# The first norm's chain, the gate weights and the order of the head stages of an mLSTM and sparse-attention trunk

## The chip, the cores and the metric

The kernel runs on one core of a Trainium2 chip. The metric is the device time of one execution in microseconds (us), as the median of several runs. Engines are named by their short names in the profile: PE is TensorE, DVE is VectorE, ACT is ScalarE, POOL is GpSimd, SP is SyncE; PEld is TensorE's weight load.

## The reference, cut to what matters

Two layers work on x of 256 tokens by 1024 channels, each as x + mixer(rmsnorm(x)); a last RMSNorm follows. The change lies in layer 0, an mLSTM block with 4 heads of 512 channels:

```python
x_in, z = split(rmsnorm(x) @ w_in)               # 1024 -> 2048 + 2048
x_conv = silu(conv4(x_in) + conv_b)              # 4 taps per channel, causal
q, k, v = headwise(x_conv, w_q), headwise(x_conv, w_k), headwise(x_in, w_v)   # 4x4 blocks
gates = concat([q, k, v]) @ w_if + b_if          # 8 gates per token
hh = mlstm(q, k, v, gates); y = (layernorm(hh) * ln_w + skip * x_conv) * silu(z)
x = x + y @ w_out
```

Layer 1 is attention with compressed, selected and window branches. All of it is float32.

## The kernel before, in words

**Products.** A product of float32 matrices is made of three products of parts: each operand is split into a high part (`hi`, `hh`, which ScalarE rounds) and the rest (`lo`, `hl`, which VectorE subtracts), and high by high, high by low and low by high are added up in PSUM (`project_channels`, L402). The weights come in units of 1 MB, two halves each (`load_unit`, L258): SP's queue loads the raw half into one of four buffers `wr`, ScalarE writes the high part `wh` (L274), and the low part `wl` is either VectorE's (L280) or, for the halves in `BY_DMA`, a copy by ScalarE (L277) and an adding transfer from POOL's queue (L278). High and low parts have five buffers each. `next_unit` keeps the loads two units ahead of their use (`LOOK`), `ahead(N0)` starts them.

**The first norm.** x comes transposed in four pieces `xch0`. ScalarE and VectorE write its scaled parts (`scaled`, L340, lines L342 and L343) without the norm's factor. The squares and their sum `sq1` (L350 to L356, then L385) are shared out by `SQA` (squares on ScalarE, the others on POOL) and `SQP` (adds on POOL, the others on VectorE). `norm1` (L384) sums over the channels by a product with ones (L388), takes the mean and 1e-6 (L323), the power -1/2 on POOL (L325), spreads the result over all partitions by a product with two diagonal tiles `dg` (L377, L378) and gets the row scale `rb1` (L389) and its half `rb1h` (L390). `rb1` is first used where the first projection leaves PSUM (`evac_x`, L438). `rstd_of` and `token_rows` serve the second layer's norm too.

**Head stages.** A loop over 4 heads (L431) projects two units into `xin` (2 buffers), and then makes the products of this head: block-diagonal weights `bdq`, `bdv` by POOL from `bm`, a part of the constants `cst` (L398); the gate weights folded through the 4x4 blocks by VectorE (`gate_weights`, L461), a product (L463) and a reduction (L464) for v and for q of each head; four convolution taps (L476 to L487); then products L497 (q), L504 (v with its gate columns), L511 and L512 (scores and gates). `cst`, the gate weights `wif` and x itself are loaded after the first unit, each behind a one-element copy of `rb1` into the tile (L441 to L449), which holds the transfer back until `rb1` is there. x1, `sq1`, `xch0`, `wif` and `z` share three buffers of the tag `zt`.

**What sets the order.** Each engine and each queue takes its instructions in one order, fixed at compile time. It is not the order of the text alone: a list scheduler runs through the program with a time model and gives each engine, among the instructions that it holds ready, the one that stands first in the text. So work of a later unit may come before that of an earlier stage, and an instruction whose operands are late on the chip holds up all that stands behind it on its engine.

Of the kernel before, what the change touches and what calls it, by code (L numbers as in the profile page):

```python
# [9 lines left out]
F32 = mybir.dt.float32  # L10
# [50 lines left out]
N0 = 2  # L61
# [4 lines left out]
SQP = (1, 2)  # L66
XT = 'zt'
NOT_POOL = (0, 1, 2, 11)
BOTH = (15, 16, 17)
BY_DMA = [(i, 1) for i in list(range(24)) + list(range(24, 48, 2)) if i not in NOT_POOL] + [(i, 0) for i in BOTH]  # L70

# [131 lines left out]
def trunk(ctx, tc, a, out, dbg=None):  # L203
# [80 lines left out]
    plan = [(a["wi1"], i, KT, 256) for i in range(16)] + [(a["wo1"], i, 4, 512) for i in range(8)]  # L284
# [99 lines left out]
    def norm1():  # L384
# [46 lines left out]
    for h in range(NH):  # L431
        xin = T([P, 4, S + 3], tag="xin", bufs=2)
        GP.memset(xin[:, :, 0:3], 0.0)
        for u in range(2):
            def evac_x(ps, x_=xin[:, 2 * u:2 * u + 2, 3:], first=(h, u) == (0, 0)):
                if first:
                    norm1()
                V.tensor_tensor(x_, ps, spread(rb1), op=OP.mult)  # L438
            project_channels(a["wi1"], 2 * h + u, evac_x, ("px", "px", "acc1")[(2 * h + u) % 3])
            if (h, u) == (0, 0):  # L440
                V.tensor_copy(cst[:, 0:1], rb1[:, 0:1])  # L441
                nc.sync.dma_start(cst, a["cst"][:, 0:n_res])
                wifs = [T([P, 16, n // 128, 8], tag="zt", bufs=ZT, name="wif") for n in (1024, 512)]
                for t, o_, n in zip(wifs, (0, 1024), (1024, 512)):
                    V.tensor_copy(t[:, 0, 0, 0:1], rb1[:, 0:1])
                    nc.sync.dma_start(t.rearrange("p a b c -> p (a b c)"), a["wif"][:, o_:o_ + n])
                for i in range(2):
                    V.tensor_copy(xt[i][:, 0, 0:1], rb1[:, 0:1])
                    nc.sync.dma_start(xt[i], a["x"][:, i * 512:(i + 1) * 512].rearrange("(t p) c -> p t c", p=P))  # L449
        if h == 0:  # L450

            wqk = CA("wqk").rearrange("p (c i) -> p c i", c=16)
            wv = CA("wv").rearrange("p (c i) -> p c i", c=16)
            atmp = T([P, 16, 4, 4], tag="f4", bufs=F4, name="atmp")
            V.tensor_tensor(atmp, CA("wkrep").rearrange("p (c i j) -> p c i j", c=16, i=4),
                            wqk[:, :, 0:4, None].to_broadcast([P, 16, 4, 4]), op=OP.mult)
            AT = T([P, 16, 4], name="AT")
            V.tensor_reduce(AT, atmp.rearrange("p c i j -> p c j i"), axis=AX.X, op=OP.add)
        own = slice(4 * h, 4 * h + 4)

        def gate_weights(out, wgt, wif, nq):  # L461
            tmp = T([P, 4, nq * 4, 8], tag="wtmp", bufs=2)
            V.tensor_tensor(tmp, wif[:, own, :, :], wgt[:, own, :, None].to_broadcast([P, 4, nq * 4, 8]), op=OP.mult)  # L463
            V.tensor_reduce(out, tmp.rearrange("p c i g -> p c g i"), axis=AX.X, op=OP.add)  # L464

        bdq = blockdiag(AT[:, own, :], F32)
        bdv = blockdiag(wv[:, 4 * h:4 * h + 4, :], F32, PG)
        gate_weights(bdv[:, :, P:PG], wv, wifs[1], 1)
# [23 lines left out]
        gate_weights(q[:, :, S:SG], wqk, wifs[0], 2)  # L492
# [27 lines left out]

    ident_r = TS([P, P], F32R, name="ident_r")
# [124 lines left out]
    for h in range(NH):  # L646
        z = T([P, 4, S], tag="zt", bufs=ZT, name="z")
        for u in range(2):
# [75 lines left out]
    nc.sync.dma_start(pkb, a["pkb"])  # L724
# [419 lines left out]
```

## Time and profile before

| | us |
|---|---|
| median of 3 runs | 381.38 (380.86 to 384.1) |
| profiled execution | 378.87 |
| its span, first to last instruction | 377.1 |
| PE busy | 350.6 (93%) |
| DVE busy | 255.7 (68%) |
| ACT busy | 241.5 (64%) |
| POOL busy | 134.7 (36%) |

Times in rows are from the start of the span. Busy PE is time in which at least one product is in flight; products are pipelined, so that the time of one is longer than the distance to the next. Idle time of an engine that is not the bound costs nothing by itself. A row of the timeline may join several instructions (xN), and its duration is then that of all.

### The profile page before, as it was taken

Reading aid. Unit: us, or ns where it says so; the run is one execution under the profiler, and the core shown is the slowest. Engines: PE = TensorE matmul, PEld = TensorE weight load, DVE = VectorE, ACT = ScalarE, POOL = GpSimd, SP = SyncE. Lnnn points to the kernel's source line nnn. Section 1 sums busy time; section 2 is a strip of 40 time slices with the busy share of each in tenths; the row PEclk is TensorE's granted clock in tenths of the full one; section 3 lists DMA queues with packets and bytes.
Section 4 is the critical chain, followed back from the end, with each engine's and each line's share of the span. In section 5 each row is a group of like instructions: output and inputs, shape, how many; then the busy total and the mean of one; then the engine's idle time right before and its main releaser. Section 6 shows DMA issues by size and latency. Waiting matters only on the chain.

```text
span 377.1 us, 6621 instructions
## 1 busy us (share of the span) xinstructions
PE 350.6 (93%) x2399; PEld 313.8 (83%) x2399; DVE 255.7 (68%) x535; ACT 241.5 (64%) x438; POOL 134.7 (36%) x165
## 2 busy tenths in 40 slices
PE   6998799979999979999999799999879999999991
PEld 6998799869998968988887699999869996777771
DVE  5976999756476548983243736687979789684515
ACT  6674669738468649765653744372579789996304
POOL 5226377433301124610100303283430283857003
PEclk9999899999999999999999999999989999999997
DMA  7889758765646978999998897546577865020003
GB/s 260 280 269 315 209 129 217 188 152 125 167 157 159 197 210 217 228 233 296 239 262 239 266 343 216 173 104 155 154 195 209 246 237 158 2 56 2 2 0 112
DMA packets 21633, 69.57 MB, mean 185 GB/s; under 512 B 2528, under 2 KB 2912, under 8 KB 21600
## 3 DMA queue, kind: packets, MB, share of 16 engines
q1 hardware_dynamic: 15472, 48.71, 38.7%
q0 software_dynamic: 4752, 16.83, 24.6%
q10 hardware_dynamic: 1376, 3.61, 2.9%
q8 instruction: 19, 0.31, 0.3%
q14 instruction: 14, 0.11, 0.1%
HBM read 50.87 MB, written 1.05 MB: 138 GB/s over the span
## 4 chain that ended last, share of the span: by engine, by line
PE 39%; DMA 23%; DVE 18%; issue 8%; ACT 8%; POOL 1%; SPq 1%; ACTq 0%; POOLq 0%; DVEq 0%
PE ps L411 17%; DMA wl<-wr 7%; DMA wr<-in_wo_dram 6%; DVE xc L487 6%; PE ps L694 6%; DVE wl L280 4%; DMA wr<-in_wi2z_dram 3%; DMA wr<-in_wi2k_dram 2%; ACT wh L274 2%; PE ps L984 2%; PE ps L909 2%; PE ps L897 2%; DMA cst<-in_cst_dram 2%; DMA xch<-in_xt_dram 1%; ACT wl L277 1%
## 5 line engine op out<-in xcount | busy, mean ns | idle before, releaser
L411 PE MATMUL ps<-hT,wh 128*128 128x256 f32 x832 | 139.5, 293 | 2.4 <-DVE hT L343 1.3
L274 ACT ACTIVATE wh<-wr 128x1024 fp32r<-128x1024 f32 (+2 forms) x90 | 89.5, 1000 | 58.1 <-PE ps L411 21.5
L411 PEld LDWEIGHTS ps<-hT,wh 128*128 128x128 f32 x832 | 121.8, 198 | 4.6 <-DVE hT L343 1.9
L280 DVE TENSOR_TENSOR wl<-wr,wh 128x1024 fp32r<-128x1024 f32 (+2 forms) x57 | 70.9, 1244 | 36.0 <-ACT wh L274 33.2
L411 PE MATMUL ps<-hT,wl 128*128 128x256 f32 x416 | 87.7, 287 | 0.0
L411 PEld LDWEIGHTS ps<-hT,wl 128*128 128x128 f32 x416 | 66.4, 193 | 1.0 <-issue 0.6
L278 POOL DMA_DIRECT2D wl<-wr x33 | 28.7, 877 | 107.9 <-ACT wl L277 103.5
L277 ACT ACTIVATE wl<-wr 128x1024 fp32r<-128x1024 f32 (+1 forms) x33 | 33.8, 1025 | 13.4 <-PE ps L694 6.6
L694 PE MATMUL ps<-wh,r 128*128 128x512 f32 x128 | 41.4, 398 | 0.0
L487 DVE SCALAR_TENSOR_TENSOR xc<-xin,pka,xc 128x256 f32<-128x256 f32 x44 | 30.8, 754 | 0.1
L694 PEld LDWEIGHTS ps<-wh,r 128*128 128x128 f32 x128 | 24.0, 188 | 5.5
L694 PE MATMUL ps<-wl,r 128*128 128x512 f32 x64 | 25.3, 395 | 0.0
L694 PE MATMUL ps<-wh,y 128*128 128x512 f32 x64 | 21.8, 406 | 0.0
L803 POOL TENSOR_TENSOR swap<-swap,trig 128x512 f32<-128x512 f32 x6 | 10.2, 1697 | 18.9 <-DMA swap<-qu 7.3
L775 PE MATMUL ps<-wl,hT 128*128 128x280 f32 (+1 forms) x48 | 15.8, 330 | 1.2 <-DMA wl<-wr 1.2
L846 PE MATMUL ps<-ka,qt 128*128 128x256 f32 (+1 forms) x32 | 12.0, 380 | 3.8 <-DVE nm L852 3.7
L774 PE MATMUL ps<-wh,hT 128*128 128x280 f32 (+1 forms) x48 | 15.5, 329 | 0.0
L776 PE MATMUL ps<-wh,hT 128*128 128x280 f32 (+1 forms) x48 | 15.2, 325 | 0.0
L694 PEld LDWEIGHTS ps<-wh,y 128*128 128x128 f32 x64 | 11.8, 188 | 3.1 <-issue 0.8
L694 PEld LDWEIGHTS ps<-wl,r 128*128 128x128 f32 x64 | 12.0, 188 | 2.8 <-DMA wl<-wr 0.2
L641 POOL TENSOR_TENSOR xc<-xc,pka 128x1024 f32<-128x1024 f32 x4 | 9.8, 2455 | 12.2 <-PE ps L512 12.2
L504 PE MATMUL ps<-m,xin 128*128 128x136 f32 x64 | 9.7, 299 | 3.6 <-DVE m L464 3.5
(473 smaller groups left out, 676.0 us busy)
## 6 DMA issues: line engine op xcount, KB each, us to landing
wr<-in_wi_dram SPq DMA_DIRECT2D x34, 512.0 KB
wl<-wr POOLq DMA_DIRECT2D x31, 512.0 KB, 5.9
wr<-in_wo_dram SPq DMA_DIRECT2D x24, 512.0 KB
wr<-in_wi2k_dram SPq DMA_DIRECT2D x12, 512.0 KB
wr<-in_wi2z_dram SPq DMA_DIRECT2D x8, 512.0 KB
wr<-in_wi2v_dram SPq DMA_DIRECT2D x8, 280.0 KB
cw<-in_cw_dram ACTq DMA_DIRECT2D x4, 512.0 KB
xch<-in_xt_dram SPq DMA_DIRECT2D x4, 256.0 KB
```

The costliest lines, as they stand in the source:

```text
L274: A.activation(hi[:, k, :], raw[:, k, :], AF.Copy)
L277: A.activation(lo[:, k, :], raw[:, k, :], AF.Copy, scale=-1.0)
L278: GP.dma_start(out=lo[:, k, :].rearrange("p k n -> p (k n)"), in_=raw[:, k, :].rearrange("p k n -> p (k n)"), accum_op=OP.add)
L280: V.tensor_tensor(lo[:, k, :], raw[:, k, :], f32(hi[:, k, :]), op=OP.subtract)
L411: PE.matmul(ps[:, c, :], w, (hl if i == 1 else hh)[:, k, :], start=(k, c, i) == (0, 0, 0), stop=(k, i) == (KT - 1, 2), skip_group_check=True)
L487: V.scalar_tensor_tensor(xc[:, c, :], xin[:, c, tap:tap + S], tap_w(tap, c), xc[:, c, :], op0=OP.mult, op1=OP.add)
L694: PE.matmul(acc, l, r[:, k % 2, cols], start=first and i == 0, stop=last and i == 2)
L774: PE.matmul(o_, lh, hi[:, k % 2, :], start=kt == 0, stop=False)
L775: PE.matmul(o_, lh, lo[:, k % 2, :], start=False, stop=False)
L776: PE.matmul(o_, ll, hi[:, k % 2, :], start=False, stop=kt == KT - 1)
L803: (GP, V)[RE[1]].tensor_tensor(sw, sw, turn(1), op=OP.mult)
L846: PE.matmul(o_, lq, ka[:, g, :, 0:w_], start=True, stop=False)
```

## The change

Squares: all four on ScalarE, after the scaled parts, their adds on VectorE. `norm1` stands ahead of the first projection, and of the loads of the second unit (`N0` is 1) and of `pka`. In it the mean goes from VectorE to ScalarE, the diagonal tiles to POOL, the half to ScalarE. `cst` and `wif` are released by `sq1` in place of `rb1`; x and `pkb` are loaded in the third head's projection. The gate weights of all heads are folded at once (`fold`), with two products and two reductions on VectorE, and POOL copies each head's part. Projections (A) and products (B) of the heads become stages of their own in the order of `STAGES`. Two casts go from VectorE to POOL. `silu_z1` is there and not called.

```diff
-N0 = 2
+N0 = 1
-SQP = (1, 2)
+SQP = ()
+XTH = 2
+WI1 = range(16)
+STAGES = "A0 A1 B0 A2 B1 A3 B2 B3"
...
-        V.tensor_scalar(me, ms, 1.0 / n, 1e-6, op0=OP.mult, op1=OP.add)
+        A.activation(me, ms, AF.Copy, scale=1.0 / n, bias=1e-6)
...
-    nc.sync.dma_start(pka, a["pka"])
...
+    scaled(range(KT), lambda kt: xch0[kt // 4][:, kt % 4, :], gain1)
     sq1 = T([P, 4, S], tag="zt", bufs=ZT, name="sq1")
...
-        (A.activation(o_, x_, AF.Square) if q in SQA else GP.tensor_tensor(o_, x_, x_, op=OP.mult))
+        A.activation(o_, x_, AF.Square)
         if q:
             (GP if q in SQP else V).tensor_tensor(sq1[:, 0:2, :], sq1[:, 0:2, :], o_, op=OP.add)
-    scaled(range(KT), lambda kt: xch0[kt // 4][:, kt % 4, :], gain1)
...
-            V.tensor_scalar(dg[:, tb, :], ident, r[:, tb:tb + 1], None, op0=OP.mult)
+            GP.tensor_scalar(dg[:, tb, :], ident, r[:, tb:tb + 1], None, op0=OP.mult)
...
-        V.tensor_scalar(rb1h, rb1, 0.5, None, op0=OP.mult)
-
+        A.activation(rb1h, rb1, AF.Copy, scale=0.5)
+
+    norm1()
+    ahead(2)
+    nc.sync.dma_start(pka, a["pka"])
...
+    def heads_x(h):
+        xin = xins[h] = T([P, 4, S + 3], tag="xin", bufs=2)
         GP.memset(xin[:, :, 0:3], 0.0)
         for u in range(2):
-            def evac_x(ps, x_=xin[:, 2 * u:2 * u + 2, 3:], first=(h, u) == (0, 0)):
-                if first:
-                    norm1()
+            def evac_x(ps, x_=xin[:, 2 * u:2 * u + 2, 3:]):
                 V.tensor_tensor(x_, ps, spread(rb1), op=OP.mult)
             project_channels(a["wi1"], 2 * h + u, evac_x, ("px", "px", "acc1")[(2 * h + u) % 3])
             if (h, u) == (0, 0):
...
+                small_weights()
+        if h == XTH:
+            V.tensor_copy(pkb[:, 0:1], xin[:, 0, 3:4])
+            nc.sync.dma_start(pkb, a["pkb"])
+            for i in range(2):
+                V.tensor_copy(xt[i][:, 0, 0:1], xin[:, 0, 3:4])
+                nc.sync.dma_start(xt[i], a["x"][:, i * 512:(i + 1) * 512].rearrange("(t p) c -> p t c", p=P))
...
+    def small_weights():
+
+        wifs = [T([P, 16, n // 128, 8], tag="zt", bufs=ZT, name="wif") for n in (1024, 512)]
+        V.tensor_copy(cst[:, 0:1], sq1[:, 0, 0:1])
+        for t, o_, n in zip(wifs, (0, 1024), (1024, 512)):
+            V.tensor_copy(t[:, 0, 0, 0:1], sq1[:, 0, 0:1])
+            nc.sync.dma_start(t.rearrange("p a b c -> p (a b c)"), a["wif"][:, o_:o_ + n])
+        nc.sync.dma_start(cst, a["cst"][:, 0:n_res])
...
+        def gate_weights(wgt, wif, nq, name):
+            out = T([P, 16, 8], name=name)
+            tmp = T([P, 16, nq * 4, 8], tag="f4", bufs=F4, name="wtmp")
+            V.tensor_tensor(tmp, wif, wgt[:, :, :, None].to_broadcast([P, 16, nq * 4, 8]), op=OP.mult)
+            V.tensor_reduce(out, tmp.rearrange("p c i g -> p c g i"), axis=AX.X, op=OP.add)
+            return out
...
+    def heads_products(h):
         if h == 0:
...
+            fold()
+        xin = xins.pop(h)
...
-        gate_weights(bdv[:, :, P:PG], wv, wifs[1], 1)
+        bdq = blockdiag(folded["AT"][:, own, :], F32)
+        bdv = blockdiag(folded["wv"][:, own, :], F32, PG)
+        GP.tensor_copy(bdv[:, :, P:PG], folded["gv"][:, own, :])
...
-        gate_weights(q[:, :, S:SG], wqk, wifs[0], 2)
+        GP.tensor_copy(q[:, :, S:SG], folded["gq"][:, own, :])
...
+    for stage in STAGES.split():
+        {"A": heads_x, "B": heads_products, "Z": silu_z1}[stage[0]](int(stage[1]))
+
     ident_r = TS([P, P], F32R, name="ident_r")
-    V.tensor_copy(ident_r, ident)
+    GP.tensor_copy(ident_r, ident)
     maskt_r = T([P, 2, P], F32R, name="maskt_r")
-    V.tensor_copy(maskt_r, C("maskt")[:, None, :].to_broadcast([P, 2, P]))
+    GP.tensor_copy(maskt_r, C("maskt")[:, None, :].to_broadcast([P, 2, P]))
...
-    nc.sync.dma_start(pkb, a["pkb"])
```

## Rows read from the trace of the kernel before

**Rows 1.** Stages: start:end length, busy us (instructions) per engine, PEclk, DMA share, GB/s
```profile
6.00:14.00 8.00, 6.53 (x28) 5.94 (x29) 8.00 (x12) 7.34 (x14) 4.49 (x3) 1.00 1.00 364
14.00:36.00 22.00, 22.00 (x187) 22.00 (x186) 16.38 (x29) 12.84 (x18) 7.84 (x7) 1.00 0.85 264
36.00:40.00 4.00, 0.51 (x6) 0.34 (x4) 4.00 (x5) 0.00 (x0) 4.00 (x4) 1.00 0.69 277
40.00:46.00 6.00, 6.00 (x38) 6.00 (x39) 6.00 (x14) 4.84 (x9) 1.11 (x2) 0.72 0.87 210
...
77.00:80.00 3.00, 0.60 (x4) 0.45 (x3) 3.00 (x6) 0.00 (x0) 1.31 (x1) 1.00 0.87 187
```

**Rows 2.** TensorE's waits: line, releaser, us in total, times, longest
```profile
PE ps L504 <- DVE m L464: 3.5, 1, 3.5
PE ps L497 <- DVE gsc L516: 2.4, 1, 2.4
```

**Rows 3.** Chain of waits from 16 to 40 us: start, us, what
```profile
25.97 6.04 DMA cst<-in_cst_dram
...
32.33 4.75 DVE xc L487 x4
37.08 2.45 DVE wtmp L463 x2
```

**Rows 4.** Stages for TensorE alone: length, PE busy, PEclk, DMA share, GB/s
```profile
42.00:44.00 2.00, 2.00 (x11) 0.50 1.03 205
```

**Rows 5.** Timelines of DVE and POOL, norm chains: start, us, engine line, operation, out<-in
```profile
14.80 0.43 DVE L385 TENSOR_TENSOR sq<-sq 128x256 f32<-128x256 f32 x1
18.51 1.63 POOL L325 TENSOR_TENSOR r<-r1me,mhalf 128x2 f32<-128x2 f32 x1 [7.01 <-DVE r1me L323]
20.17 0.48 DVE L377 TENSOR_SCALAR dg<-pk,r 128x128 f32<-128x128 f32 x2 [0.61 <-POOL r L325]
24.53 0.42 DVE L389 COPY rb<-ps 128x256 f32<-128x256 f32 x1 [1.37 <-PE ps L378]
...
210.35 1.48 DVE L323 TENSOR_SCALAR r2me<-r2ms 128x2 f32<-128x2 f32 x1
```

**Rows 6.** Timelines of SP's queue and of ACT, third and fourth unit
```profile
14.19 2.53 SPq L273 DMA_DIRECT2D wr<-in_wi_dram  x2
...
20.84 1.06 ACT L274 ACTIVATE wh<-wr 128x1024 fp32r<-128x1024 f32 x1 [1.86 <-DMA wr<-in_wi_dram]
```

**Rows 7.** Single lines on VectorE: count, shortest/median/longest ns, first and last start, forms
```profile
L463 DVE TENSOR_TENSOR wtmp<-wif,pka x8: 279/413/1477, 37.0 to 49.5; 128x128 f32<-128x128 f32 x4, 128x256 f32<-128x256 f32 x4
L464 DVE TENSOR_REDUCE m<-wtmp x4: 360/366/398, 39.5 to 56.9; 128x32 f32<-128x128 f32 x4
L464 DVE TENSOR_REDUCE q<-wtmp x4: 597/634/650, 39.7 to 51.4; 128x32 f32<-128x256 f32 x4
...
L280 DVE TENSOR_TENSOR wl<-wr,wh x21: 677/1217/2804, 6.4 to 118.3; 128x1024 fp32r<-128x1024 f32 x17, 128x512 fp32r<-128x512 f32 x4
```

**Rows 8.** A small POOL line, in the same columns
```profile
L508 POOL TENSOR_TENSOR gva<-gva,v x4: 313/1040/1681, 47.6 to 91.1; 128x64 f32<-128x64 f32 x4
```

**Rows 9.** Timelines of DVE and ACT in the first 12 us
```profile
5.61 0.87 DVE L343 SCALAR_TENSOR_TENSOR hT<-xch,pk,hT 128x256 fp32r<-128x256 f32 x2
6.41 1.52 DVE L280 TENSOR_TENSOR wl<-wr,wh 128x512 fp32r<-128x512 f32 x1
7.85 1.89 DVE L343 SCALAR_TENSOR_TENSOR hT<-xch,pk,hT 128x256 fp32r<-128x256 f32 x2
9.10 0.63 ACT L354 ACTIVATE sq<-xch 128x512 f32<-128x512 f32 x1
10.27 1.90 DVE L343 SCALAR_TENSOR_TENSOR hT<-xch,pk,hT 128x256 fp32r<-128x256 f32 x2
```

**Rows 10.** Timelines of DVE and POOL before the wait at 77 us
```profile
73.40 5.99 DVE L487 SCALAR_TENSOR_TENSOR xc<-xin,pka,xc 128x256 f32<-128x256 f32 x3
75.64 2.66 POOL L534 TENSOR_TENSOR vsp<-v,vsp 128x1024 fp32r<-128x1024 f32 x1
```

More of the change, by code (lines that the diff above doesn't have):

```diff
@@ L282, in load_unit @@
         return halves
-    plan = [(a["wi1"], i, KT, 256) for i in range(16)] + [(a["wo1"], i, 4, 512) for i in range(8)]
+    plan = [(a["wi1"], i, KT, 256) for i in WI1] + [(a["wo1"], i, 4, 512) for i in range(8)]
     of_step = {"v": [(a["wi2v"], i, 4, 280) for i in range(4)], "c": [(a["wi2"], i, 4, 512) for i in range(2)]}
@@ L430, in trunk @@
     convw = CA("convw").rearrange("p (t c) -> p t c", t=4)
-    for h in range(NH):
-        xin = T([P, 4, S + 3], tag="xin", bufs=2)
+    xins, zt_ = {}, {}
+    def heads_x(h):
+        xin = xins[h] = T([P, 4, S + 3], tag="xin", bufs=2)
         GP.memset(xin[:, :, 0:3], 0.0)
         for u in range(2):
-            def evac_x(ps, x_=xin[:, 2 * u:2 * u + 2, 3:], first=(h, u) == (0, 0)):
-                if first:
-                    norm1()
+            def evac_x(ps, x_=xin[:, 2 * u:2 * u + 2, 3:]):
                 V.tensor_tensor(x_, ps, spread(rb1), op=OP.mult)
@@ L440, in trunk @@
             if (h, u) == (0, 0):
[L441 to L449, printed above, removed]
@@ L450, in trunk @@
-        if h == 0:
[L452 to L458, printed above, removed]
@@ L459, in trunk @@
-        own = slice(4 * h, 4 * h + 4)
[L461 to L467, printed above, removed]
-        gate_weights(bdv[:, :, P:PG], wv, wifs[1], 1)
+                small_weights()
@@ new lines, in heads_x @@
+        if h == XTH:
[4 more added lines that the diff above has]
+                nc.sync.dma_start(xt[i], a["x"][:, i * 512:(i + 1) * 512].rearrange("(t p) c -> p t c", p=P))
+    folded = {}
+    def small_weights():
[5 more added lines that the diff above has]
+        nc.sync.dma_start(cst, a["cst"][:, 0:n_res])
+        folded["wif"] = wifs
@@ new lines, in fold @@
+    def fold():
+        wifs = folded["wif"]
+        wqk = CA("wqk").rearrange("p (c i) -> p c i", c=16)
+        wv = CA("wv").rearrange("p (c i) -> p c i", c=16)
+        atmp = T([P, 16, 4, 4], tag="f4", bufs=F4, name="atmp")
+        V.tensor_tensor(atmp, CA("wkrep").rearrange("p (c i j) -> p c i j", c=16, i=4),
+                        wqk[:, :, 0:4, None].to_broadcast([P, 16, 4, 4]), op=OP.mult)
+        AT = T([P, 16, 4], name="AT")
+        V.tensor_reduce(AT, atmp.rearrange("p c i j -> p c j i"), axis=AX.X, op=OP.add)
+        def gate_weights(wgt, wif, nq, name):
[4 more added lines that the diff above has]
+            return out
+        folded.update(AT=AT, wv=wv, gv=gate_weights(wv, wifs[1], 1, "gwv"), gq=gate_weights(wqk, wifs[0], 2, "gwq"))
@@ L519, in trunk, with silu_z1, evac_z @@
         scs.append(sc)
+    def silu_z1(h):
+        z = zt_[h] = T([P, 4, S], name="z")
+        for u in range(2):
+            def evac_z(ps, z=z[:, 2 * u:2 * u + 2, :]):
+                V.tensor_tensor(z, ps, spread(rb1), op=OP.mult)
+                A.activation(z, z, AF.Silu)
+            project_channels(a["wi1"], 8 + 2 * h + u, evac_z)
+    for stage in STAGES.split():
+        {"A": heads_x, "B": heads_products, "Z": silu_z1}[stage[0]](int(stage[1]))
     ident_r = TS([P, P], F32R, name="ident_r")
-    V.tensor_copy(ident_r, ident)
+    GP.tensor_copy(ident_r, ident)
     maskt_r = T([P, 2, P], F32R, name="maskt_r")
-    V.tensor_copy(maskt_r, C("maskt")[:, None, :].to_broadcast([P, 2, P]))
+    GP.tensor_copy(maskt_r, C("maskt")[:, None, :].to_broadcast([P, 2, P]))
     causal = C("mask2")
@@ L646, in trunk @@
     for h in range(NH):
-        z = T([P, 4, S], tag="zt", bufs=ZT, name="z")
-        for u in range(2):
+        z = zt_[h] if h in zt_ else T([P, 4, S], tag="zt", bufs=ZT, name="z")
+        for u in range(0 if h in zt_ else 2):
             def evac_z(ps, z=z[:, 2 * u:2 * u + 2, :]):
```

## The prediction

> **What bounds the kernel now.** I read the table of stages first, cut where TensorE's idle time lies: it shows that the kernel is held by TensorE nearly everywhere (22.00 of 22.00 us between 14 and 36 us) and that three stretches of the region that the change edits have holes: 6 to 14 us (6.53 of 8), 36 to 40 us (0.51 of 4) and 77 to 80 us (0.60 of 3) [rows 1]. What an edit is worth is read from these holes. The list of TensorE's waits says what ended the two deep ones: L504 (the products of head 0 with the value weights) waited 3.5 us for the gate weights of L464, and L497 waited 2.4 us for a PSUM bank that VectorE's `gsc` add at L516 had to free [rows 2].
>
> The chain of waits through 26 to 40 us then shows why L464 was late: the 6.04 us of the `cst` load, issued at 25.97 us only, since it is held back until the row scale `rb1` exists; then 4.75 us for four convolution steps, 2.45 us for the two gate products [rows 3]. The stall has a second price. After it the granted clock is 0.72 of full speed over the six us from 40 to 46 [rows 1], with 0.50, that is 1.2 of 2.4 GHz, in all of 42 to 44 us [rows 4]; in the stretches before it is 1.00. Lost work: 6 x 0.28 = 1.7 us. So the hole before head 0 costs 3.5 + 1.7 = 5.2 us. The shorter one at 77 us was not followed by a lower clock.
>
> **The change part by part.**
>
> *Loads of `cst` and `wif` tied to the squares, behind the third unit's.* Before, both wait for `rb1`, done at 24.95 us [rows 5]; after, their gate is the sum of squares `sq1`, whose last add ended at 15.2 us [rows 5]. On SP's queue they now stand behind the third unit's second half, which issued right at 14.19 us, and ahead of the fourth unit's, which before followed at about 16 to 18 us [rows 6]. So they issue near 15 to 17 us. With `cst`'s own 6.04 us from issue to landing [rows 3] they are there at about 21 to 23 us, some 9 us sooner than 32.0. Fold, block-diagonal weights and gate copies for head 0 then need: two gate instructions and their POOL work, about 5 us, so L504's operands are ready at 27 to 30 us. TensorE comes to L504 at about 35 us, being full of units 1 to 4 until then. Margin 5 us or more: **the 3.5 us stall goes, and the 1.7 us of lower clock with it: 5.2 us.** What is late next is the fourth unit, behind 1.02 MB more (128 partitions of 1536 and 456 words). At the 264 GB/s of that stretch [rows 1] that is 3.9 us. Its first half was converted at 20.84 us [rows 6], and TensorE began that unit at about 31 us (it ran dry at 36.5, less 48 products at 187 in 22 us [rows 1]): some 10 us in hand, so I put it at nothing. Its last half is tighter, as its low part goes through a further POOL transfer; that bounds a loss at 0 to 2 us. The loads of x and `pkb` (1.1 MB) move out of this crowded stretch to the third head's, which pays part of it back.
>
> *The fold.* Eight products (0.28 and 0.41 us at their usual) and eight reductions (0.37 and 0.63 us) become four: worked out from the sizes, products at 0.68 and 1.22 us (L280 has the same sizes), reductions at about 1.2 and 2.2 us (0.63 less 0.37 per 128 elements more) [rows 7]. 5.3 us against 6.8: 1.5 us less VectorE work. More to the point, it moves from VectorE's full stretch, 36 to 57 us, into 14 to 36 us, where VectorE was busy 16.38 of 22 us [rows 1]. Eight gate copies on POOL come in, 0.31 us each at the least [rows 8], 2.5 us in all, beside the products: nothing on the path.
>
> *Squares on ScalarE, POOL's adds to VectorE.* POOL's two squares and two adds leave. Between 6 and 12 us they stretched VectorE: L280 took 1.52 us where 0.68 is its least for that size, a pair of L343 took 1.89 us where another one took 0.87, and another pair 1.90 [rows 7, 9]: 0.84 + 1.02 + 1.03 = 2.9 us lost on the engine that feeds the first products. But ScalarE, busy 7.34 of 8 us there [rows 1], gets two more squares of 0.63 us [rows 9], 1.26 us, ahead of or behind the last `hT`. Between 1.3 us lost and 1.8 us gained I take 0.8 us: the last inputs land near 9.5 us anyway, and the ordering is open, the scaled copies being emitted first.
>
> The Trainium skill (SBUF — State Buffer, Who interferes with whom) says that a VectorE instruction with two SBUF inputs and a GpSimd instruction that reads SBUF exclude each other whole, which the rows of 1.52 and 1.89 us bear out. By that rule alone the front would give back all 2.9 us instead of 0.8, and the sum would be 9.3 us.
>
> *The chain to the row scale, emitted first.* The mean and 1e-6 go to ScalarE, the two diagonal products to POOL (VectorE did them in 0.48 us [rows 5]; POOL's row for the power is 1.63 us, so 0.5 to 3.3 us), the halved copy to ScalarE. TensorE does not wait for `rb1` as such: from 14 to 36 us it is full although `rb1` comes at 24.95 us. So the earlier scale alone is worth nothing; what it brings is an earlier first convolution. The same helpers serve the second norm near 212 us, where the mean on VectorE took 1.48 us [rows 5]; moving the mean away from there and adding POOL's slower products I bound at -1 to +1 us and take 0. The two casts that go to POOL are off the path.
>
> *The order A0 A1 B0 A2 B1 A3 B2 B3.* It puts the next head's projections ahead of a head's products. TensorE's real order was already so in the first four units, so the early part is unchanged; later it gives VectorE more time per head.
>
> *The stall at 77 us.* Three convolution steps took 5.99 us beside POOL instructions that stay, one of them of 2.66 us [rows 10]. Nothing here removes them; only their place changes. Bounds 0 and 2.4 us; I take the middle, 1.2.
>
> Sum: 5.2 + 0.8 + 1.2 = 7.2 us. The profiled execution took 378.87 us, span 377.1 and 1.8 around it: 369.9 span, 371.7 us in all. The median of the runs is 381.38 us, 2.5 above that execution; on it the forecast is **374.2 us**. After 110 us TensorE is again the bound, and the weight loads follow its releases of buffers, so I let the gain pass.
>
> **Rivals.**
>
> *More goes than I count.* Front 1.8 us, both later holes whole: 5.2 + 1.8 + 2.4 = 9.4 us, 372.0 us, and to 369.5 us if the second norm's wait goes as well. For it: VectorE's load falls in all of 14 to 57 us. Against: POOL's long instructions remain.
>
> *A new wait takes the place of the old.* Either VectorE copies that release `wif` and `cst` are queued late, so that the loads hardly come sooner (then the change does not do what it says), or `wif` is late at the fold and holds up the conversions queued behind it on VectorE, as the convolution at 32.33 us came only behind `cst` [rows 3]; or the fourth unit's low half is 2 us late and the clock falls again, 1.7 us. 3 to 6 us of the 7.2 are lost: 377.4 to 380.5 us, taken as 379.
>
> *TensorE is held by the scale chain (the slower side).* L388 and L378 are now emitted ahead of the first unit's products. TensorE takes its queue in order. If L378 is queued soon after L388, everything behind it waits for ScalarE's mean, POOL's power and POOL's diagonals. Before, with these spread out, it was 9.7 us from the sum of squares (15.2) to `rb1` (24.95) [rows 5], and TensorE waited for none of it. Were all of it waited for, with 1.7 us of clock after it, that is 11.4 us against 7.2 gained: 385.6 us. Without queueing, the chain's own steps (power 1.63, diagonals 0.5 to 3.3, mean and products about 1.5) are 4 to 6 us. It makes the kernel slower from 7.2 us of waiting on. Against it: the products of unit 1 have their data in the same stretch and would have to be ordered behind for no reason.
>
> **How the numbers follow.** Chances: forecast 0.55 (its own range 371.5 to 377.5 us), more goes 0.15, a new wait 0.20, held by the scale chain 0.10. 1% is about what a measurement of this kernel can tell from no change: 377.6 and 385.2 us. Faster: the first two but a little, 0.66. Slower: half of the last and some unforeseen disorder downstream, 0.09, as the whole order of instructions is laid out anew. The same: 0.25. The range, 369.5 to 381.5 us, takes in the first three and leaves out the last and a tail.
>
> **What would show it.** Right: no wait of L504 over 1 us, granted clock 1.00 through 36 to 46 us, `cst` landed before 24 us, `rb1` before 21 us, VectorE's first L343 pairs near 0.9 us, TensorE past the last L504 some 6 to 8 us sooner. Wrong: a TensorE wait at L388, L378 or at L411 for ScalarE's copies of unit 4; a clock of 0.5 anywhere before 60 us; or the head stage's gain lost again in the waits at L615 or past 200 us.

## The result and the profile after

| | before | after |
|---|---|---|
| median of 4 runs each | 381.12 us (379.45 to 384.1) | 389.12 us (387.03 to 390.16) |
| profiled execution | 378.87 us | 388.65 us |
| its span | 377.1 us | 386.9 us |
| PE, DVE, ACT, POOL busy | 350.6, 255.7, 241.5, 134.7 us | 354.9, 247.2, 243.4, 128.4 us |

The ratio is 1.028, 95% interval 1.022 to 1.033: slower by 8 us, where 374.2 us were forecast and 381.5 was the upper end of the range. Medians are of all runs, ratios of the fast ones alone (a run counts as slow when it is over 1.5% above the fastest of its kernel; in e3 and e6 below these are two of four). Table of stages of the changed kernel, with the columns of [rows 1]: first that group's stretches, then the ones in which the time went.

```profile
6.00:14.00 8.00, 6.12 (x31) 5.92 (x32) 7.02 (x13) 7.34 (x15) 0.00 (x0) 0.61 0.96 360
14.00:36.00 22.00, 17.98 (x137) 17.81 (x137) 16.91 (x22) 13.29 (x19) 12.33 (x18) 0.89 0.83 272
36.00:40.00 4.00, 4.00 (x26) 4.00 (x26) 1.89 (x2) 1.64 (x3) 2.15 (x2) 0.68 0.88 209
40.00:46.00 6.00, 6.00 (x53) 6.00 (x52) 4.56 (x7) 5.59 (x10) 2.77 (x4) 1.00 0.58 158
77.00:80.00 3.00, 3.00 (x22) 2.79 (x21) 1.82 (x2) 2.71 (x4) 1.11 (x2) 1.00 0.75 262
84.00:104.00 20.00, 18.69 (x145) 17.93 (x144) 13.19 (x16) 10.93 (x18) 9.06 (x6) 1.00 0.36 95
160.00:200.00 40.00, 36.33 (x156) 27.92 (x155) 11.97 (x15) 22.14 (x28) 5.11 (x6) 1.00 0.95 254
210.00:220.00 10.00, 6.07 (x25) 4.70 (x24) 3.86 (x6) 6.60 (x13) 4.36 (x7) 0.80 0.93 303
```

The last three stretches of the kernel before, which the prediction did not read:

```profile
84.00:104.00 20.00, 20.00 (x155) 19.43 (x154) 10.71 (x15) 13.21 (x21) 6.15 (x6) 1.00 0.61 142
160.00:200.00 40.00, 40.00 (x182) 32.31 (x181) 18.37 (x23) 24.71 (x31) 6.00 (x7) 1.00 0.99 260
210.00:220.00 10.00, 8.36 (x54) 7.38 (x53) 6.80 (x14) 6.84 (x13) 3.19 (x5) 1.00 0.99 300
```

The reader is to see three things. The holes at 36 to 40 and 77 to 80 us are gone, but one of 4 us stands in 14 to 36. In 160 to 200 us, the out-projection, TensorE was full before (182 products) and now makes 156. And there the DMA engines were as full as TensorE already before: 0.99. The changed kernel's waits of TensorE (engine, tile, line, releaser: us in total, times, longest) name the same places:

```profile
PE ps L418 <- DVE xin L445: 4.0, 1, 4.0
PE ps L811 <- ACT hT L346: 3.9, 1, 3.9
PE ps L418 <- ACT wh L279: 3.2, 3, 1.6
PE ps L732 <- DMA wl<-wr: 2.9, 4, 1.4
```

How the time went, by the start of the first ("begins") or of the last ("ends") of TensorE's instructions of a stage (us):

| | before | after | difference |
|---|---|---|---|
| head 0's value products begin | 40.0 | 41.2 | +1.2 |
| last scores end | 100.4 | 97.3 | -3.1 |
| out-projection begins | 156.9 | 155.9 | -1.0 |
| out-projection ends | 203.2 | 206.5 | +3.3 |
| diagonals of the second norm end | 213.6 | 220.5 | +6.9 |
| second layer's keys begin | 269.1 | 280.6 | +11.5 |
| last product ends | 369.0 | 378.7 | +9.7 |

The heads were 3 us early at 97 us. The loss came later, where nothing had been edited but two helpers: 2.1 us up to the out-projection, 4.3 in it, 3.6 from there to the diagonals and 2.8 in the second layer. The prediction had named a gain lost again "past 200 us" as a sign of being wrong.

### The profile page after: what moved, and what is told of

The parts are those of the page before. It is cut to its first block, busy times and chain, and to the rows that moved or that the text cites. A ratio compares the mean times of both kernels' runs of the same rounds, so it can differ in the third digit from the quotient of the medians.

```text
span 386.9 us, 6634 instructions
## 1 busy us (share of the span) xinstructions
PE 354.9 (92%) x2399; PEld 316.8 (82%) x2399; DVE 247.2 (64%) x517; ACT 243.4 (63%) x443; POOL 128.4 (33%) x175
## 4 chain that ended last, share of the span: by engine, by line
PE 57%; DMA 16%; DVE 11%; ACT 7%; issue 6%; SPq 1%; ACTq 0%; POOLq 0%; POOL 0%; DVEq 0%
PE ps L418 27%; DMA wl<-wr 6%; PE ps L732 5%; DMA wr<-in_wi_dram 4%; DMA wr<-in_wo_dram 3%; DVE wl L285 3%; ACT wh L279 2%; PE ps L653 2%; PE ps L537 2%; PE ps L1021 2%; PE ps L946 2%; PE ps L530 2%; PE ps L934 2%; PE ps L523 2%; DMA xch<-in_xt_dram 1%
## 5 line engine op out<-in xcount | busy, mean ns | idle before, releaser
L418 PE MATMUL ps<-hT,wh 128*128 128x256 f32 x832 | 139.0, 294 | 8.6 <-DVE xin L445 4.0
L418 PEld LDWEIGHTS ps<-hT,wh 128*128 128x128 f32 x832 | 121.9, 199 | 11.1 <-issue 6.3
L285 DVE TENSOR_TENSOR wl<-wr,wh 128x1024 fp32r<-128x1024 f32 (+2 forms) x57 | 67.4, 1186 | 47.2 <-ACT wh L279 45.1
L418 PE MATMUL ps<-hT,wl 128*128 128x256 f32 x416 | 88.9, 289 | 1.1 <-ACT p__495_2879 L891 1.1
L418 PEld LDWEIGHTS ps<-hT,wl 128*128 128x128 f32 x416 | 67.6, 195 | 2.0 <-ACT p__495_2879 L891 1.5
L732 PE MATMUL ps<-wh,r 128*128 128x512 f32 x128 | 41.2, 398 | 0.8 <-DVE x L754 0.8
L513 DVE SCALAR_TENSOR_TENSOR xc<-xin,pka,xc 128x256 f32<-128x256 f32 x44 | 29.1, 723 | 4.3 <-ACT xc L502 2.5
L811 PE MATMUL ps<-wh,hT 128*128 128x280 f32 (+1 forms) x48 | 16.4, 352 | 3.9 <-ACT hT L346 3.9
L812 PE MATMUL ps<-wl,hT 128*128 128x280 f32 (+1 forms) x48 | 16.7, 350 | 0.0
L840 POOL TENSOR_TENSOR swap<-swap,trig 128x512 f32<-128x512 f32 x6 | 8.3, 1384 | 24.6 <-DMA swap<-kraw 12.6
L813 PE MATMUL ps<-wh,hT 128*128 128x280 f32 (+1 forms) x48 | 15.7, 339 | 0.0
L811 PEld LDWEIGHTS ps<-wh,hT 128*128 128x128 f32 x48 | 9.5, 201 | 5.2 <-ACT hT L346 4.4
L732 PE MATMUL ps<-wl,y 128*128 128x512 f32 x32 | 12.8, 401 | 0.0
```

The lines of the kernel that those rows point to most:

```text
L285: V.tensor_tensor(lo[:, k, :], raw[:, k, :], f32(hi[:, k, :]), op=OP.subtract)
L418: PE.matmul(ps[:, c, :], w, (hl if i == 1 else hh)[:, k, :], start=(k, c, i) == (0, 0, 0), stop=(k, i) == (KT - 1, 2), skip_group_check=True)
L513: V.scalar_tensor_tensor(xc[:, c, :], xin[:, c, tap:tap + S], tap_w(tap, c), xc[:, c, :], op0=OP.mult, op1=OP.add)
L732: PE.matmul(acc, l, r[:, k % 2, cols], start=first and i == 0, stop=last and i == 2)
L811: PE.matmul(o_, lh, hi[:, k % 2, :], start=kt == 0, stop=False)
L812: PE.matmul(o_, lh, lo[:, k % 2, :], start=False, stop=False)
```

## The experiments

Ratios are to the kernel before on the same chip, with 95% intervals (its median there: 378.36 us for e1 to e4, 378.27 for e5 to e8, 379.88 for e9 to e12, 380.6 for e13 to e16). Theories: A, the second norm's helpers cost the time; F, the order of stages and these helpers do together; H, the order by itself; S, the out-projection is bound by its weight stream; W, the early stall is the fold's wait for `wif` on VectorE's queue. The letters in the expectations that are not listed here are explained where they stand.

**e1, second norm's helpers back** (in the changed kernel)

```diff
-        A.activation(me, ms, AF.Copy, ...)
+        V.tensor_scalar(me, ms, ...) if name == "r2" else A.activation(...)
-            GP.tensor_scalar(dg[:, tb, :], ident, ...)
+            (V if place else GP).tensor_scalar(dg[:, tb, :], ident, ...)
```

> The changed kernel, but in the second norm the mean and the two diagonal tiles go back to VectorE; every engine's order ahead of that norm is the changed kernel's own. Theory A (the helpers that both norms share cost the loss at the second norm: ScalarE's mean stands behind a conversion that waits for a load, POOL's diagonals take 1.2 us, and the clock falls): TensorE's idle time near 213 to 217 us falls from about 4.9 to 1 to 2 us, no stretch at 0.50, and the kernel takes 381 to 384 us, 5 to 8 less than the changed one. Theory B (the loss comes from the weight stream being late ahead of the second norm): 387 to 389 us, TensorE still idle there, waiting for what a load brings.

Measured 388.97 us (387.91 to 392.07), 1.030 [1.022, 1.038]. The diagonals ended at 215.0 instead of 220.5 us, and the keys began at 276.4 instead of 280.6; and yet nothing reached the end: the second layer came out of the list scheduler in another order, in which the keys take 77.2 us instead of 70.9 and the values end at 373.3 instead of 370.0. A alone falls as to the total.

**e2, the helpers alone** (the same two edits the other way round, in the kernel before)

> The kernel before, but in the second norm the mean goes to ScalarE and the diagonal tiles to POOL; the order ahead of that norm is the kernel before's own. Theory A: slower than before by 5 to 8 us (386 to 389), with a longer wait of TensorE at the diagonal product of the second norm and a lower clock behind it. Theory B: 380 to 383 us.

Measured 381.82 us, 1.012 [1.004, 1.021]: the helpers cost about 1% even without the rest, not the 5 to 8 us that A had asked for.

**e3, fold per head** (the changed kernel with the old products and reductions of each head)

```diff
-            tmp = T([P, 16, nq * 4, 8], tag="f4", ...)      # all heads, once
+            tmp = T([P, 4, nq * 4, 8], tag="wtmp", bufs=2)  # one head
...
-        GP.tensor_copy(bdv[:, :, P:PG], folded["gv"][:, own, :])
+        gate_weights(bdv[:, :, P:PG], folded["wv"], wifs[1], 1)
```

> The changed kernel with the gate weights folded head by head as before (eight products and eight reductions, written straight to their places), all else of it kept. Theory C (the fold of all heads, queued on VectorE ahead of the first three projections' leaving of PSUM, costs the 4.0 us wait and the lower clock at 29 to 40 us): the wait for xin before head 0's products falls under 1.5 us, the head stage ends 4 to 6 us sooner. If what is gained there lasts: 383 to 385 us. Theory D (weight loads or the second norm decide the time behind it, so that gains of the head stage do not last): 387 to 390 us with the head stage sooner.

Measured 389.22 us (384.04 to 392.04), 1.021 [1.008, 1.034]. Head 0's value products began at 34.0 us, 7 us earlier. So the early stall is the fold's, and taking it away in this manner brings nothing that can be told from noise.

**e4, old order of the stages** (in the changed kernel)

```diff
-STAGES = "A0 A1 B0 A2 B1 A3 B2 B3"
+STAGES = "A0 B0 A1 B1 A2 B2 A3 B3"
```

> The changed kernel with the order A0 B0 A1 B1 A2 B2 A3 B3 as the loop before had it, all else kept. If the new order is what helps the head stage (its last products were 3 us sooner than before in spite of the wait at 29 us): 390 to 393 us. If it is neutral: 388 to 390. If it is what puts the fold and the weights in a bad order: 383 to 386.

Measured 381.46 us, 1.007 [1.002, 1.012]: 2% of the 2.8% come back with one line, and they do so ahead of the second layer: the diagonals of the second norm end at 211.3 us instead of 220.5. It is more than was expected, 383 us at the least.

**e5, old order and helpers back** (e4 and e1)

> The changed kernel with the old stage order and with the second norm's mean and diagonals back on VectorE. Theory F (two harmful parts, each with its own loss: the stage order some 2% and the second norm's engines some 1%, and the rest of the change gains in the head stage): 374 to 378 us against 378.4 before on this chip, ratio 0.985 to 1.00, and 3 us less than with the order alone put back. Theory G (what is put right at the second norm is lost again in the newly laid out second layer, as when it alone was put back): the same as with the order alone put back, ratio 1.00 to 1.01.

Measured 377.2 us, 0.996 [0.992, 1.000]. F holds: without these two parts the change is level with the kernel before or a little under it. Against e4 (381.46) the helpers are worth 1%, though in e1 they gave nothing.

**e6, new order alone** (the kernel before, its loop cut into A and B)

```diff
-    for h in range(NH):
+    def heads_x(h): ...
+    def heads_products(h): ...
+    for stage in "A0 A1 B0 A2 B1 A3 B2 B3".split(): ...
```

> The kernel before with nothing but the order A0 A1 B0 A2 B1 A3 B2 B3 of the head stages. Theory H (projections first bunch the use of weights and leave a stretch of two heads' products in which no weight buffer comes free, the loads pause, and the out-projection, bound by the weight stream, starts with less in hand): 1.5 to 2.5% slower than before, a stretch near 85 to 100 us with a DMA share under 0.3, and TensorE waits in the out-projection. Theory I (the order is harmful only together with the fold): within 0.7% of before.

Measured 394.7 us (388.35 to 397.18), 1.032 [1.023, 1.041]. The order alone makes the kernel before slower, by about as much as the whole change does. But only 3.7 us of it are there at the diagonals of the second norm (217.3 against 213.6 us); of the 14.6 us at the last product, 10.9 come in the second layer, which has the longer order of e1 (keys 79.1 us). H's figure for the pause, a DMA share under 0.3, was missed: 0.40.

**e7, head 0's z units between B2 and B3** (in the changed kernel; their SiLU becomes one instruction in it):

```diff
-STAGES = "A0 A1 B0 A2 B1 A3 B2 B3"
+STAGES = "A0 A1 B0 A2 B1 A3 B2 Z0 B3"
```

> The changed kernel with the first gate-path stage (two weight units, its SiLU as one function) put between the products of heads 2 and 3: weights are used in the stretch that had none. Theory H: the DMA share at 85 to 100 us rises from 0.2 to over 0.5 and 3 to 7 us are gained on the changed kernel (382 to 386). Theory J (the pause of the loads does not matter, as they are ahead of their use): within 2 us of the changed kernel's 389.

Measured 383.9 us, 1.012 [1.005, 1.019], 5 us less than the changed kernel. 84 to 104 us in e6, then in e7:

```profile
84.00:104.00 20.00, 18.70 (x141) 17.77 (x140) 13.47 (x18) 11.65 (x21) 9.53 (x7) 1.00 0.40 106
```

```profile
84.00:104.00 20.00, 20.00 (x157) 19.53 (x156) 12.88 (x13) 12.08 (x20) 7.88 (x6) 1.00 0.50 138
```

With two product stages side by side no weight buffer comes free and the loads pause: DMA share 0.40 in e6 and 0.36 after, against 0.61 before. A weight stage between them brings it to 0.50.

**e8, e5 with the fold per head**

> The changed kernel with the old stage order, the old second norm and the gate weights folded head by head. The 4 to 5 us wait of TensorE for xin at 29 to 33 us is the fold's, so that it falls under 1.5 us in any case. If the fold's wait is what is left of the loss: 2 to 5 us less than with the order and the norm alone put back, 371 to 375 us. If VectorE's backlog takes it back later, as it did in the changed kernel with its own order (TensorE's lag 7.4 us at 40 us, but 17 at 80): the same as without it, within 2 us.

Measured 386.26 us, 1.020 [1.013, 1.026]. Its out-projection began at 151.5 us, 3.3 earlier than that of e5, and ended at 202.4, 0.8 later, with three waits for `wl`; the rest of its loss lies in the second layer, which has the longer order of e1 again (keys 79.1 us). Neither expectation came: it is 2.4% over e5. Being early brought nothing. That pointed to what the out-projection is fed by. By queue in 160 to 200 us (packets, MB, share of the 16 engines' time), of the changed kernel:

```profile
q1 hardware_dynamic: 1836, 6.67, 47.9%
q0 software_dynamic: 943, 3.46, 46.5%
```

q1 carries the loads, q0 GpSimd's adding transfers, which make `wl` for the halves in `BY_DMA`. They hold the engines for 5.4 us per MB (0.465 x 40 us / 3.46 MB), the loads for 2.9 (0.479 x 40 / 6.67). The changed kernel's chain of waits through that stretch (start, us, what) is mostly one transfer after another:

```profile
158.03 7.23 DMA wl<-wr
165.31 7.30 DMA wr<-in_wo_dram
...
175.06 5.22 DMA wr<-in_wo_dram
...
181.73 7.64 DMA wl<-wr
...
189.84 8.79 DMA wr<-in_wi_dram
...
201.29 7.88 DMA wl<-wr
```

and so it was in the kernel before, while TensorE was full:

```profile
167.58 5.79 DMA wl<-wr
173.43 3.77 DMA wr<-in_wo_dram
...
180.13 5.85 DMA wl<-wr
186.04 3.36 DMA wr<-in_wo_dram
...
191.12 8.07 DMA wl<-wr
199.21 8.38 DMA wr<-in_wi2k_dram
```

**e9, e10, e11: the low parts of six second halves by VectorE**, in e5, in the changed kernel and in the kernel before:

```diff
-NOT_POOL = (0, 1, 2, 11)
+NOT_POOL = (0, 1, 2, 11, 18, 19, 20, 21, 22, 23)
```

> The changed kernel with the old stage order and the second norm's helpers back on VectorE (as in e5_order_norm_back), and the low parts of the second halves of the out-projection's weight units 2 to 7 (18 to 23 of the list) made by VectorE instead of GpSimd's accumulating DMA. In e5 the DMA engines are full in 160 to 200 us and TensorE's waits in the out-projection are for wl by a DMA. Theory S (the out-projection is bound by what the DMA engines carry, and the accumulating DMAs are part of it): the out-projection, 46.8 us from its first to its last instruction in e5, takes 43.5 to 45.5, the waits L732 <-DMA wl go from 2.9 us each to under 1, and the time is 0.99 to 0.995 of e5's, about 374. Rival (it is bound by the weight loads from HBM themselves, or VectorE has no room there): the out-projection stays within 0.7 us, and the time is within 0.5% of e5's; if VectorE has no room, the waits change their name to DVE and it is 1 to 2% slower.

> The changed kernel, with the low parts of the second halves of the out-projection's weight units 2 to 7 made by VectorE instead of GpSimd's accumulating DMA, nothing else. Theory S: the out-projection, 50.6 us in the changed kernel, takes 46 to 48; about 2.5 us of that reaches the end, 385 to 387 us. Rival (the loads alone bind it): 50 to 51 and 388 to 390.

> The kernel before, with the low parts of the second halves of the out-projection's weight units 2 to 7 made by VectorE instead of GpSimd's accumulating DMA, nothing else. In the kernel before TensorE is busy 10.0 of every 10 us in 160 to 200 us: nothing there waits for a load. Theory S: within 0.5% of before, since there is no wait to take away. Rival (the accumulating DMAs also delay the loads behind them): 1% faster.

Measured: e9 373.65 us, 0.984 [0.977, 0.992]; e10 378.96, 0.999 [0.995, 1.003]; e11 375.23, 0.988 [0.980, 0.997]. One line takes 2.8% off the changed kernel, with the new order and the new helpers kept. As it takes 1.2% off the kernel before as well (e11), some 1.7 of the 2.8% that the change had cost went through this stream. Against e11, e10 is still 1% slower (378.96 to 375.23 us): the two are level at the diagonals (209.4 and 209.9 us), and e10 loses in the second layer. The stages and queues of e10:

```profile
160.00:200.00 40.00, 39.47 (x175) 31.81 (x174) 21.32 (x22) 20.77 (x27) 0.86 (x1) 1.00 0.70 225
210.00:220.00 10.00, 10.00 (x68) 9.23 (x67) 4.53 (x10) 5.30 (x9) 0.00 (x0) 1.00 0.95 318
```

```profile
q1 hardware_dynamic: 2188, 7.94, 56.8%
q0 software_dynamic: 281, 1.02, 13.0%
```

The DMA share falls from 0.95 to 0.70 though the loads carry more (7.94 MB for 6.67), TensorE's products go from 156 to 175, and of TensorE's waits from 200 to 225 us one of 0.7 us is left, at full clock. The Trainium skill (DMA: Bandwidth & Descriptors, Issuing engines are not separate DMA queues) says that transfers started by ScalarE, SyncE or GpSimd run on the same 16 DMA engines and interleave there. The two queues' shares, which add up to that of the engines, agree with it. Three sizes missed: e10 gained 10 us where 2.5 were expected; e9's out-projection did not get shorter than e5's (48.3 us against 46.8; its gain lies behind it, in 210 to 220 us and in the second layer), and e11 gained the rival's 1% (1.2%) where theory S had none, behind the out-projection: it ends at 202.9 us (203.2 before), but the second norm's diagonals at 209.9 (213.6), as the loads that follow it had waited in the same stream (the 8.38 us above).

**e12, the fold behind head 0's x** (in e5)

```diff
             tmp = T([P, 16, nq * 4, 8], tag="f4", bufs=F4, name="wtmp")
+            V.tensor_copy(tmp[:, 0, 0, 0:1], xins[0][:, 2, 3:4])
             V.tensor_tensor(tmp, wif, ...)
```

> As e5_order_norm_back (old stage order, second norm's helpers on VectorE), and the fold's products tied behind the conversion of the first head's second x unit, so that VectorE does not stand at the wait for wif with the copy of rb and the conversions of xin behind it. Theory W (the wait for wif at the head of VectorE's queue is what stops TensorE for 6.3 us at 27 to 33 us): that wait falls under 1.5 us, the clock stays at 0.8 or more in 30 to 40 us where it was 0.6, and the diagonals of head 0 come 0 to 3 us earlier; of the 5 us, 2 to 5 reach the end if nothing later takes them, 372 to 375. Rival G (the gain is given back at the out-projection, as in e8): the early stall goes, the first norm's loop and the heads are 3 to 5 us earlier at 150 us, the out-projection takes longer by as much, and the time is within 0.5% of e5's.

Measured 385.71 us, 1.015 [1.005, 1.025]. The stall went (30 to 40 us: TensorE 10.00 of 10 at clock 1.00, where e5 has 6.75 at 0.66). The out-projection began at 148.6 us, 6.2 earlier than e5's, and ended at 198.6, 3.0 earlier: it took 50.0 us instead of 46.8, with four waits for `wl`. The other half went in the second layer, which has the longer order here (keys 79.4 us, 73.7 in e5). So the fold's place on VectorE's queue makes the stall, as W says, though its wait for `wif` does not (next section). G was right that the gain is given back, but it was given back at two places, and it did not end level.

**e13, both** (e12 with the line of e9); **e14**, e9 with the new order; **e15**, e13 with the second halves of units 16 and 17 and the first halves of 15 to 17 on VectorE too; **e16**, e13 with the new order.

> The changed kernel with the old stage order, the second norm's helpers on VectorE, the fold tied behind the conversion of the first head's second x unit (as in e12), and the low parts of the second halves of weight units 18 to 23 on VectorE (as in e9). Theory S (the out-projection's weight stream took the gain of e12, whose stages up to 150 us were 5 us earlier than those of e9): the gain now reaches the end of the out-projection, which ends at 197 to 199 us against 201.8 in e9, and the time is 368 to 371. Rival: the time goes back to that of e9, 373 to 375, because the loads themselves bind the out-projection's start, or because the second layer's list comes out in the longer layout (above 377).

> The changed kernel with its own stage order, the second norm's helpers back on VectorE, and the low parts of the second halves of weight units 18 to 23 on VectorE: e9 with the new order. Theory S (the order costs only because it brings the out-projection into its weight stream): within 0.5% of e9, 372 to 376, and about 3 us under e10 for the helpers. Rival H (the order costs 2% by the loads that pause at 84 to 104 us, whatever comes later): 1.5 to 2% over e9, 379 to 381.

> As e13, with all low parts of weight units 16 to 23, and the first halves of unit 15, on VectorE: GpSimd's accumulating DMAs end with the second half of unit 15. Theory S: the DMA share in 150 to 200 us falls further below 0.75, and the out-projection, at 45 to 47 us, does not get shorter than in e13 by more than 1 us, since TensorE has no wait for wl left there; the time is within 0.5% of e13. Rival V (VectorE has no room for six more passes between 130 and 165 us, where it is busy nine tenths): conversions of the heads wait, and it is 1% slower than e13.

> As e13, with the changed kernel's own stage order. Theory S: within 0.5% of e13. Rival H: 1.5 to 2% over e13. The fold sits behind the first head's x here too, so the stall at 29 to 33 us of the changed kernel should be gone, and the clock in 30 to 40 us 0.8 or more.

| | us | ratio |
|---|---|---|
| e13 | 370.45 (367.82 to 371.44) | 0.975 [0.969, 0.982] |
| e14 | 376.2 (373.95 to 376.6) | 0.992 [0.988, 0.995] |
| e15 | 370.92 (369.11 to 372.76) | 0.976 [0.970, 0.982] |
| e16 | 374.44 (371.44 to 376.12) | 0.986 [0.979, 0.993] |

The stretch in e13:

```profile
160.00:200.00 40.00, 39.62 (x175) 31.91 (x174) 21.54 (x24) 21.33 (x27) 0.85 (x1) 1.00 0.66 210
```

e13 has the lowest median, with e15 level. Against e9 the fold's edit brings head 0's value products from 39.2 to 35.6 us, the end of the out-projection from 201.8 to 198.0 and the last product from 365.2 to 361.3: with the light stream its gain is there at the end (3.2 us by the medians). (Against e12 most of the difference is the second layer's order, which is the short one again, keys 72.6 us.) A still lighter stream (e15, share 0.56) brings no more. The new order costs 0.7% (e14 against e9) and 1.1% (e16 against e13) with the light stream, against 2% (e4) with the full one: between S and H. The intervals of e14 and e9, and of e16 and e13, overlap, so this remainder is likely, not shown. Up to the diagonals it is 0.8 and 0.7 us (209.6 against 208.8, 205.7 against 205.0), where e4 had 9.2: to there S holds.

## Why the prediction was wrong, step by step

**"`cst` and `wif` ... are there at about 21 to 23 us": some 4 us late, `wif` at 25.9, `cst` at 26.5.** The gate, the sum of squares, came later, not sooner: with all squares on ScalarE behind its scaled copies, the last add ended at 16.8 us (15.2 in [rows 5]), and the releasing copies came at 18.4, behind a reduction and a weight subtraction on VectorE. VectorE's timeline of the changed kernel (start, us, line, operation, out<-in):

```profile
16.40 0.42 DVE L389 TENSOR_TENSOR sq<-sq 128x256 f32<-128x256 f32 x1
16.73 0.60 DVE L476 TENSOR_REDUCE AT<-atmp 128x64 f32<-128x256 f32 x1
17.26 1.21 DVE L285 TENSOR_TENSOR wl<-wr,wh 128x1024 fp32r<-128x1024 f32 x1
18.39 0.14 DVE L461 COPY cst<-sq 128x1 f32<-128x1 f32 x1
...
25.20 1.23 DVE L285 TENSOR_TENSOR wl<-wr,wh 128x1024 fp32r<-128x1024 f32 x1 [4.25 <-ACT wh L279]
26.35 2.67 DVE L481 TENSOR_TENSOR wtmp<-wif,pka 128x512 f32<-128x512 f32 x2
28.94 0.41 DVE L393 COPY rb<-ps 128x256 f32<-128x256 f32 x1
29.27 1.04 DVE L482 TENSOR_REDUCE gwv<-wtmp 128x128 f32<-128x512 f32 x1
30.24 1.99 DVE L482 TENSOR_REDUCE gwq<-wtmp 128x128 f32<-128x1024 f32 x1
32.15 1.87 DVE L445 TENSOR_TENSOR xin<-ps,rb 128x512 f32<-128x512 f32 x3
```

and SP's queue, where both stand behind the fourth unit's loads, and one half of the fifth's, instead of ahead of them:

```profile
13.27 5.56 SPq L278 DMA_DIRECT2D wr<-in_wi_dram  x4
18.88 1.82 SPq L464 DMA_DIRECT2D wif<-in_wif_dram  x2
20.74 0.43 SPq L465 DMA_DIRECT2D cst<-in_cst_dram  x1
```

**"The 3.5 us stall goes, and the 1.7 us of lower clock with it": the first half held, and a new one took its place.** L504 (now L530) waits no more, 40 to 46 us is at clock 1.00, and the fold's 5.7 us (2.67 + 1.04 + 1.99) are near the 5.3 forecast. But the fold is queued on VectorE ahead of the copy of `rb` and of the first three conversions of `xin`: `rb1` came at 29.4 us, where under 21 was the sign of being right, and TensorE stood 4.0 us at L418 for a PSUM bank, then ran at the lower clock, 0.50, to 38.5 us. That cost 2.8 us, half of the 5.5 us in which it was busy at it. Not all of `rb1`'s delay is the fold's: TensorE took up the sum's product (L392) at 21.2 us, 4.4 after the sum, and in e13, with the fold behind, `rb1` comes at 26.3.

This is the second rival's "`wif` is late at the fold and holds up the conversions queued behind it on VectorE", right in the queue and wrong in the lateness. VectorE's waits from 18 to 34 us are one, for ScalarE's high part of a weight half:

```profile
DVE wl L285 <- ACT wh L279: 4.2, 1, 4.2
```

`wif` was there before the subtraction behind that wait had ended, and the fold began right after it, without a wait. In e13 the same wait stands (3.9 us) and TensorE's is 0.3. So what held up the conversions was the fold's own 5.7 us, and `wif` at 22 us would not have helped in this queue. The rival's price was put at 3 to 6 us, and 4.0 + 2.8 = 6.8 were paid. e12 and e13 showed it by taking it away. The rival's time (377.2 to 380.2 by its own terms, not 377.4 to 380.5) would have been that of e5: 0.996 of the kernel before, some 380 us on the forecast's scale.

**Squares and front, 0.8 us: right sign, too small.** Its upper end of 1.8 us follows from no row (2.9 less 1.26 is 1.6), and 0.8 is not the middle of its bounds. POOL's work is gone from 6 to 14 us, and pairs of L347 take 0.88 us (1.89 in [rows 9]). In e5, whose front is the same, TensorE makes 95 products from 6 to 20 us, against 78 before: 17 x 22/187 = 2.0 us. The profiled execution of the changed kernel has 78 too: it ran at clock 0.50 from 8 to 14 us. By the rule of the Trainium skill on shared access (SBUF — State Buffer, Who interferes with whom) the front would have given back 2.9 us; e5's 2.0 lie between that and the 0.8.

**The stall at 77 us, 1.2 of 2.4: it went whole** (3.00 of 3 us busy).

**The order "gives VectorE more time per head", at no cost: failed.** It puts two product stages side by side, and the loads, which follow TensorE's release of weight buffers, pause there (0.36 against 0.61). I moved this step past TensorE and VectorE, and not past SP's queue. Worth 2% in this kernel (e4); by itself (e6) 3.7 us up to the second norm, and the rest of its 3.2% in the second layer's order.

**The second norm's helpers, "-1 to +1 us and take 0": failed.** ScalarE's timeline of the changed kernel shows the mean (0.19 us where VectorE took 1.48, [rows 5]; at the first norm the same line of VectorE took 0.15) queued behind a copy for `wl` that waits for its load:

```profile
213.90 1.06 ACT L282 ACTIVATE wl<-wr 128x1024 fp32r<-128x1024 f32 x1 [1.88 <-DMA wr<-in_wi2k_dram]
214.37 0.89 ACTq L1005 DMA_DIRECT2D cw<-in_cw_dram  x2
214.87 0.19 ACT L328 ACTIVATE r2me<-r2ms 128x2 f32<-128x2 f32 x1
```

The mean's input was there at 212.2. POOL's two diagonals then took 1.20 us (0.48 on VectorE). The price is 1% (e2, and e5 against e4). The hole follows from the stream as well: in e10, helpers as after, the diagonals end at 209.4 us, and in e14, which differs from e10 in the helpers alone, at 209.6. Even so e14 is 0.7% faster (376.2 against 378.96 us). All six kernels with these helpers in the second norm (after, e2, e3, e4, e7, e10) have a wait of TensorE of 2.2 to 2.9 us in the second layer, for VectorE's `kcb` (L1044 in the changed kernel), and no other has more than 1.3. So their price is in part one of the new order of that layer.

**"After 110 us TensorE is again the bound ... so I let the gain pass": the step that decided.** TensorE was full in 160 to 200 us and the DMA engines were too. In these runs an earlier arrival there was given back in part or nearly whole, and a disturbed stream (the pause at 84 to 104 us) stops TensorE. Of their lead over the kernel before, from the begin to the end of the out-projection, e5 kept 1.6 of 2.1 us, e4 2.6 of 5.6, e12 4.6 of 8.3 and e8 0.8 of 5.4. The out-projection took 46.3 us before and 46.8 in e5; in seven others with the full stream (after, e1, e2, e4, e6, e8, e12) it took 49.3 to 51.4, with waits for `wl`, whether it began early or late; with the light stream (e9 to e11, e13 to e16) 46.0 to 48.3. (e7's 52.1 us are another case: no wait for `wl`, but one of 2.7 us for VectorE at 158 us and the lower clock behind it.) With the light stream the change without its order and its second norm, and with the fold moved, is worth 1.3% (e13 against e11, 370.45 against 375.23; their intervals overlap, but their second layers have the same order and their diagonals end at 205.0 and 209.9 us): some 4.8 of the 7.2 us forecast.

**The slower side** was given 0.09, by TensorE held at the scale chain and by unforeseen disorder downstream. The disorder came. No wait at L392 or L382 stands in the first norm, so that rival fell. A rival "the out-projection has no room" was missing, and the stage table of before, read past 110 us, would have given it.

What stays open: the second layer, which nobody edited, came out in three orders. From the diagonals to the last product it took 155 to 159 us without a wait for `kcb` (before, e5, e9, e11, e13 to e16), 158 to 160 with the wait of 2.2 to 2.9 us, and 164 to 169 in e1, e6, e8 and e12 (keys 77 to 79 us, 70 to 74 in the others). The list scheduler's answer to small shifts is part of each of these times, and was not isolated: most of the 3.2% of e6 and of the difference between e12 and e13 is its.

Nor is it shown whether the DMA engines themselves bind the out-projection or the buffers `wr` do. An adding transfer also keeps its raw half's buffer from issue to landing (median 6.5 us before, 7.3 in the changed kernel), where VectorE's subtraction takes 1.2, and the next load waits for that buffer. From 155 to 205 us SP's queue waited 35.5 us for such transfers in the changed kernel, 25.9 before and 18.7 in e10. The one line lightens both.

## What to carry to other kernels

Read the DMA share beside TensorE's busy time in every stage that a gain must pass through: where both are full, an earlier start can be lost there, and freeing the stream can be worth more than the edit upstream (one line gave 2.8% here, and 1.2% to the kernel before). When stages are put in another order, follow the queue of the loads through it too, and look for stretches in which no buffer comes free. Several us of work that nothing waits for yet belong behind the conversions that free PSUM on their engine, not ahead of them. And before a loss is put down to an edit, see whether the part of the kernel that nobody edited still has the same order.

## What the runs showed of the hardware

An adding transfer from SBUF to SBUF held the DMA engines, by the time of their packets, about twice as long per MB as a load from HBM (5.4 against 2.9 us; before, 52.8% for 3.67 MB against 45.5% for 6.69 MB, that is 5.8 against 2.7).

The first products of kernels that are alike up to there ran at either clock level. From 8 to 14 us it was 0.50 in the profiled executions of the changed kernel, e9, e14 and e15, in which TensorE was busy 0.66 to 0.87 of the 2 us from 4 to 6. It was 1.00 in e1, e4, e5, e7, e12, e13 and e16, with 1.19 or 1.20, and low for a part of the time (0.72) in e3, e8 and e10, also with 1.19. The lower level all the way costs some 17 products (2 us). e5 and e9 differ only in weight units 18 to 23 and stand on either side, so it does not come from the edits; what it does come from is not shown.
